# A hybrid encoder trunk on Trainium2: three edits to the order of queues around a retention stage

## The chip, the cores and the metric

The kernel runs on one core of one Trainium2 chip. A core has a matrix engine (TensorE, PE in the profile; PEld is its weight load), a vector engine (VectorE, DVE), a scalar engine (ScalarE, ACT), a general engine (GpSimd, POOL) and an engine that only issues transfers (SyncE, SP). Each works through its own list of instructions in order and waits on semaphores where an operand comes from another engine or from a transfer. The metric is the time of one execution on the device, in microseconds (us); several executions are timed and the median is given.

## The reference

Input is one sequence of 1024 frames with 1024 channels, in float32. The program has two layers, each x = x + mixer(RMSNorm(x)), and a last RMSNorm. The first layer projects h once and feeds two branches, whose gated outputs are joined by one output projection:

```python
proj = h @ w_in
u_s5, g_s5, q, k, v, g_ret = jnp.split(proj, cuts, axis=-1)
y = jax.nn.gelu(scan(u_s5))                      # S5 state-space branch
y = y * jax.nn.sigmoid(y @ glu_w + glu_b)        # its gate, a 1024 x 1024 product
y_s5 = y * jax.nn.silu(g_s5)
# retention: 8 heads, chunks of 64 frames, 64 key and 128 value channels a head
q, k = rope(q) * 64 ** -0.5, rope(k)
out = (q @ k.T * decay) @ v + (q * q_dec) @ S    # S: sum over earlier chunks of k.T @ v
out = (out - mean(out)) * rsqrt(var(out) + 1e-6) # per head
y_ret = out * jax.nn.silu(g_ret)
x = x + jnp.concatenate([y_s5, y_ret], axis=-1) @ w_out
```

(cut and shortened). The second layer is a convolution module: one projection into three parts, a causal depthwise convolution over 31 frames, a norm, and an output projection.

## The kernel before

Matrix products are made in three passes to keep float32 accuracy: each operand is split into a high part (a cast, `wh` for weights, `xh` or `yh` for data) and a low part (operand minus high part, `wl`, `xl`, `yl`), and TensorE adds high x high, low x high and high x low. A weight block comes in as one transfer (`wf`), ScalarE makes the cast, GpSimd or VectorE the subtraction. `wload_split` (L162 to L168) does it for the blocks of the value product and others, L266 to L269 for the gate's weights `glu0` to `glu7`.

The program is written in stages, and a scheduler turns them into one list per engine: it follows the order of writing and the priorities, but lets an instruction pass others that wait. `issue_after(x)` keeps all instructions written under it behind x, on x's own engine alone.

Three stages are touched. **The value product** (`ret_values`) goes over V_ORDER, seven products of combined weights; blocks are called V1_0, V1_1, V4_0 and so on (`mm_v` on TensorE, L1108 to L1110). Beside it `y_pass` (L942 to L945) takes the S5 output from DRAM (`yp`), applies the gelu on ScalarE (`yn`) and stores it to `yn_d`; these are the y norm passes, in the words of the change. Its instructions stand behind `last_sum`, the newest sum of a value product. **The key products** follow, and among them `y_operands` (L1071 to L1079), which loads the S5 output after the gelu again as eight blocks of two halves (`yf`), and splits them into `yh` and `yl`: these are the operands of the gate. **The retention** (`retention`, L947) goes over four pairs of heads. For a pair, `ret_turn` loads keys and queries from DRAM (`kraw`, `kswp`, `qraw`, `qswp` on SyncE), multiplies them by the rotary tables on GpSimd (L1004, L1006) and adds them on VectorE (L1014). `ret_heads` transposes the keys (`ktp`), decays them (`kt`), sums the states (`kv` on TensorE, `S` on VectorE), makes the scores (`sp`, masked into `sc`) and the outputs `ro0` and `ro1` of the two halves of the sequence, takes their mean and variance (`st`, `mv`), the root (`rs`, ScalarE), the normed `on` (VectorE), and transposes that back (`rt`), where it meets the gate `grl`, which is stored to `yr_d`. Names with two numbers carry the head and the half: `on_1_0` is head 1, first half.

While a pair is at work, two things are laid beside it. `glu_ahead` makes the S5 gate of the next block of 128 channels: a product of 24 matmuls a half (`mm_glu`), a tanh on ScalarE, the product `yg` on GpSimd (L1091) and the gated result on VectorE (L1095). And `weight_low` (L227 to L240) prepares low parts of weights that the second layer will need: a load (`lf`, L232), a cast on ScalarE (`lh`, L233), a subtraction on GpSimd (L234) and a store to DRAM (`lo`, L237). The four low parts of this stage, 20 to 23, have a single buffer each for `lf` and `lh`; the tuple H_LOWS says how many of them have been written when each pair begins.

## Time and profile before

| | |
|---|---|
| runs | 1177.71, 1180.71, 1185.98 us; median 1180.71 |
| profiled execution | 1179.18 us, its span from first to last instruction 1177.4 us |
| TensorE busy | 1155.9 us, 98% of the span; granted clock 0.997 on average |
| VectorE, GpSimd, ScalarE busy | 954.2, 718.3, 566.6 us (81%, 61%, 48%) |
| longest waits of TensorE | 2.4 us at `rt` of pair 0, 2.2 us at the first gate product, 2.1 us in two waits at later `rt`, 1.4 us in the value product |

Times in the views are microseconds from the start of the span. TensorE's waits are listed by the line that waited and the instruction that released it last; a stretch view gives busy time and the granted clock of the matrix engine in chosen windows. Rows of a time line say start, length, engine, line, operation and tiles; xN stands for N instructions in a row, and brackets hold the idle time ahead of the row and what ended it. A row "SPq" or "ACTq" is the issue of a transfer. The value product lies around 360 to 400 us, pair 0 of the retention begins near 500 us, pair 2 ends near 605 us.

### The profile page before, as it was taken

How to read it: one execution, taken by the hardware profiler on the slowest of the kernel's cores; microseconds unless marked ns; L12 is line 12 of the kernel's file. 1: busy time of each engine (PE TensorE's matmuls, PEld its weight loads, DVE VectorE, ACT ScalarE, POOL GpSimd, SP SyncE). 2: the span in 40 equal slices, each digit the busy share in tenths (PEclk: the TensorE clock that was granted, in tenths of full speed). 3: DMA queues.
4: the chain of work that ended last, by engine and by line, in shares of the span. 5: the costliest groups of instructions: out<-in, count | busy, mean ns of one | idle time of the engine just before them, and what ended most of it. 6: DMA issues, size and time to landing. Idle time of an engine off the chain costs nothing.

```text
span 1177.4 us, 17601 instructions
## 1 busy us (share of the span) xinstructions
PE 1155.9 (98%) x6102; PEld 958.2 (81%) x6102; DVE 954.2 (81%) x1541; ACT 566.6 (48%) x855; POOL 718.3 (61%) x499
## 2 busy tenths in 40 slices
PE   9999999999999999998999999999999999999997
PEld 7888788788887888877888788888888888888877
DVE  6889989999725666676888999579999999999643
ACT  7212342332236756413224846467756578544662
POOL 2049999888841143686532053439894689977742
PEclk9999999999999999999999999999999999999999
DMA  9359579877799979997676879975448653366863
GB/s 342 109 166 326 193 271 320 269 272 273 249 308 334 366 249 313 361 300 255 209 237 238 308 249 305 344 255 187 161 161 297 221 181 133 126 192 232 277 250 139
DMA packets 142137, 293.74 MB, mean 249 GB/s; under 512 B 14048, under 2 KB 42976, under 8 KB 141920
## 3 DMA queue, kind: packets, MB, share of 16 engines
q1 hardware_dynamic: 140896, 288.43, 72.2%
q10 hardware_dynamic: 1152, 4.19, 0.9%
q8 instruction: 48, 0.79, 0.3%
q14 instruction: 41, 0.34, 0.1%
HBM read 210.32 MB, written 81.20 MB: 248 GB/s over the span
## 4 chain that ended last, share of the span: by engine, by line
PE 70%; DVE 12%; DMA 10%; issue 3%; ACT 2%; SPq 1%; POOL 1%; DVEq 0%; ACTq 0%; POOLq 0%
PE mm_g L279 5%; PE mm_g L278 5%; PE mm_g L277 5%; PE mm_w L279 4%; PE mm_w L278 4%; PE mm_w L277 4%; PE mm_k L1026 4%; PE mm_a L279 2%; PE mm_b L278 2%; PE mm_a L278 2%; PE mm_b L279 2%; PE mm_a L277 2%; PE mm_b L277 2%; PE mm_oc L279 2%; PE mm_oc L278 2%
## 5 line engine op out<-in xcount | busy, mean ns | idle before, releaser
L1533 DVE SCALAR_TENSOR_TENSOR cv<-u,convw,cv 128x512 f32<-128x512 f32 x358 | 244.5, 748 | 4.5 <-ACT cv L1519 3.0
L1513 POOL TENSOR_TENSOR tp<-tp,tp 128x512 f32<-128x512 f32 x104 | 138.9, 1338 | 28.8 <-ACT tp L1512 23.5
L279 PE MATMUL mm_g<-xh,wl_g 128*128 128x512 f32 x256 | 100.8, 394 | 0.0
L278 PE MATMUL mm_g<-xl,wh_g 128*128 128x512 f32 x256 | 100.6, 393 | 0.0
L277 PE MATMUL mm_g<-xh,wh_g 128*128 128x512 f32 x256 | 100.4, 392 | 0.0
L1512 ACT ACTIVATE tp<-u,convw 128x512 f32<-128x512 f32 x104 | 69.8, 714 | 11.3 <-POOL tp L1513 11.0
L167 POOL TENSOR_TENSOR wl_K<-wf_K,wh_K 128x1024 fp32r<-128x1024 f32 x14 | 34.0, 2430 | 48.6 <-ACT wh_K L166 46.6
L278 PEld LDWEIGHTS mm_g<-xl,wh_g 128*128 128x128 f32 x256 | 48.1, 188 | 11.3 <-issue 1.6
L279 PEld LDWEIGHTS mm_g<-xh,wl_g 128*128 128x128 f32 x256 | 48.0, 188 | 10.5
L277 PEld LDWEIGHTS mm_g<-xh,wh_g 128*128 128x128 f32 x256 | 48.1, 188 | 9.6
L279 PE MATMUL mm_oc<-zh,wl_woc 128*128 128x512 f32 (+1 forms) x152 | 54.4, 359 | 0.6 <-DMA wl_woc<-lo_woc 0.6
L277 PE MATMUL mm_oc<-zh,wh_woc 128*128 128x512 f32 (+1 forms) x152 | 54.3, 361 | 0.0
L278 PE MATMUL mm_oc<-zl,wh_woc 128*128 128x512 f32 (+1 forms) x152 | 54.0, 356 | 0.0
L277 PE MATMUL mm_glu<-yh,wh_glu 128*128 128x512 f32 x128 | 51.2, 400 | 2.2 <-ACT yh L1270 2.2
L278 PE MATMUL mm_u<-xl,wh_u 128*128 128x512 f32 x128 | 50.0, 391 | 1.0 <-DVE xl L399 1.0
L278 PE MATMUL mm_glu<-yl,wh_glu 128*128 128x512 f32 x128 | 50.5, 394 | 0.2 <-DVE yl L1272 0.2
L279 PE MATMUL mm_glu<-yh,wl_glu 128*128 128x512 f32 x128 | 50.6, 396 | 0.0
L277 PE MATMUL mm_g<-h1h,wh_cg 128*128 128x512 f32 x128 | 50.3, 393 | 0.0
L277 PE MATMUL mm_a<-h1h,wh_ca 128*128 128x512 f32 x128 | 50.2, 392 | 0.0
L279 PE MATMUL mm_b<-h1h,wl_cb 128*128 128x512 f32 x128 | 50.2, 392 | 0.0
L279 PE MATMUL mm_a<-h1h,wl_ca 128*128 128x512 f32 x128 | 50.0, 390 | 0.0
L279 PE MATMUL mm_g<-h1h,wl_cg 128*128 128x512 f32 x128 | 49.8, 389 | 0.0
(834 smaller groups left out, 3671.9 us busy)
## 6 DMA issues: line engine op xcount, KB each, us to landing
wf_g<-w_ab SPq DMA_DIRECT2D x16, 512.0 KB, 6.2
a<-w_out SPq DMA_DIRECT2D x32, 256.0 KB, 4.5
ws<-a SPq DMA_DIRECT2D x32, 256.0 KB, 4.5
lf<-w_c SPq DMA_DIRECT2D x32, 256.0 KB, 5.1
wf_p<-ws SPq DMA_DIRECT2D x16, 512.0 KB, 4.8
wf_cb<-w_c SPq DMA_DIRECT2D x16, 512.0 KB, 5.0
wf_ca<-w_c SPq DMA_DIRECT2D x16, 512.0 KB, 4.8
wl_cb<-lo_cb SPq DMA_DIRECT2D x16, 512.0 KB, 3.3
```

The source lines that it names most:

```text
L167: e.tensor_tensor(wl[:].rearrange(fl), wf[:], wh[:].rearrange(fl).bitcast(F32), op=ALU.subtract)
L277: nc.tensor.matmul(ps, wh[:, kb, :], xh, start=start, stop=False, skip_group_check=chain)
L278: nc.tensor.matmul(ps, wh[:, kb, :], xl, start=False, stop=False, skip_group_check=chain)
L279: self.last_mm = nc.tensor.matmul(ps, wl[:, kb, :], xh, start=False, stop=stop, skip_group_check=chain)
L1026: self.last_mm = self.nc.tensor.matmul(ps, l[:, k, :], r[:], start=start and k == m == 0, stop=stop and k == 3 and m == 2, skip_group_chec ...
L1512: nc.scalar.mul(sk[:], u[:, k:k + HALF], cw[:, nb, k:k + 1])
L1513: gp.tensor_tensor(s0[:], s0[:], sk[:], op=ALU.add)
L1533: v.scalar_tensor_tensor(dst[:], *tap, accs_[i][:], op0=ALU.mult, op1=ALU.add)
```

## The change

Three edits. In `wload_split` the cast is kept as `last_cast`, and `y_pass` is written under `issue_after(last_cast)` beside `issue_after(last_sum)`: its gelu and its store on ScalarE's queue come behind the newest weight cast written so far. In `y_operands` the load is kept as `y_loaded`, and `ret_turn(pair + 1)` is written under `issue_after(y_loaded)`: SyncE issues the reload of the next pair's keys and queries behind the last load of a gate operand (only for the second pair are there such loads still to come). And H_LOWS goes from (0, 2, 4, 4) to (0, 0, 2, 4): low parts 20 and 21 are written beside the second pair instead of the first, 22 and 23 beside the third instead of the second.

```diff
--- before.py
+++ after.py
@@ -34,7 +34,7 @@
 LO_V = {f"g{i}" for i in range(1, 10)} | {"u4", "u5", "u6"}
 G0 = 3
 TP = 6
-LOWS, K_LOWS, V_LOWS, H_LOWS = 24, 20, 6, (0, 2, 4, 4)
+LOWS, K_LOWS, V_LOWS, H_LOWS = 24, 20, 6, (0, 0, 2, 4)
 NG = 4
 BLOCKS = ((4, 0), (4, 1), (0, 0), (0, 1), (1, 0), (1, 1), (5, 0), (5, 1), (2, 0), (2, 1), (3, 0), (3, 1), (6, 0), (7, 0), (6, 1), (7, 1))
 P_ORDER = ([(1, nb) for nb in range(4)] + [(2, nb) for nb in range(4)] +
@@ -163,7 +163,7 @@
         wh = self.wp.tile([P, KB, P], F32R, name=f"wh_{name}", tag="wh", bufs=3)
         wl = self.wp.tile([P, KB, P], F32R, name=f"wl_{name}", tag="wl", bufs=3)
         fl = "p k n -> p (k n)"
-        self.nc.scalar.copy(wh[:].rearrange(fl), wf[:])
+        self.last_cast = self.nc.scalar.copy(wh[:].rearrange(fl), wf[:])
         e.tensor_tensor(wl[:].rearrange(fl), wf[:], wh[:].rearrange(fl).bitcast(F32), op=ALU.subtract)
         return wh, wl
 
@@ -980,7 +980,8 @@
                     early.close()
                     self.lp = self.pool("l1", side="right")
             if pair < 3:
-                cur = self.ret_turn(pair + 1)
+                with self.tc.issue_after(self.y_loaded.ins):
+                    cur = self.ret_turn(pair + 1)
             self.ret_heads(pair, K, Q, qadds, V, turned)
             if pair < NG - 1:
                 self.glu_ahead(pair + 1)
@@ -1073,7 +1074,7 @@
 
         for kb in kbs:
             f = pool.tile([P, HALF], F32, name=f"yf{kb}_{h}", tag="xf", bufs=3)
-            self.nc.sync.dma_start(f[:], self.yn_d[kb * P:(kb + 1) * P, h * HALF:(h + 1) * HALF])
+            self.y_loaded = self.nc.sync.dma_start(f[:], self.yn_d[kb * P:(kb + 1) * P, h * HALF:(h + 1) * HALF])
             a, b = (self.op_tile(self.opA, f"A{h}", f"y{q}{kb}_{h}") for q in "hl")
             self.split(f[:], a, b, self.nc.vector)
             self.ys_in[h].append((a, b))
@@ -1148,7 +1149,7 @@
                     self.last_sum = scaled(d, h, b, ps[:], i in (3, 5))
                 for d, h in {5: ((0, 1),), 1: ((0, 0),), 6: ((0, 1),), 7: ((1, 0), (1, 1))}.get(i, ()):
                     self.last_sum = summed(d, h, b, ps[:])
-            with self.tc.issue_after(self.last_sum.ins):
+            with self.tc.issue_after(self.last_sum.ins), self.tc.issue_after(self.last_cast.ins):
                 for cb in (n - 1, n + 3) if 0 < n < 5 else ():
                     self.y_pass(vp, cb)
             with self.tc.issue_after(self.fetched.ins):
```

The scheduler's lists differ in more than these instructions. On ScalarE, in the value product, the rows below are before and then of the change (names as above; line numbers behind L982 are higher by one in the new file):

```order
L1122 CAST xh_2_1_171<-xf42_3616 128x512
L944 ACT_TABLE_LOAD
L944 ACTIVATE yn_0_3714<-yp_0_3712 128x1024
L166 CAST wh_V1_1_3680<-wf_V1_1_3678 128x1024
L945 DMA yn_d_87<-yn_0_3714 128x1024
L944 ACTIVATE yn_4_3719<-yp_4_3717 128x1024
L1122 CAST xh_3_1_181<-xf43_3620 128x512
L1122 CAST xth0_3600<-xf10_3624 128x512
L166 CAST wh_V4_0_3728<-wf_V4_0_3726 128x1024
L945 DMA yn_d_87<-yn_4_3719 128x1024
L1122 CAST xth1_3602<-xf11_3628 128x512
L166 CAST wh_V4_1_3758<-wf_V4_1_3756 128x1024
```

```order
L1123 CAST xh_2_1_171<-xf42_3616 128x512
L166 CAST wh_V1_1_3680<-wf_V1_1_3678 128x1024
L944 ACT_TABLE_LOAD
L944 ACTIVATE yn_0_3714<-yp_0_3712 128x1024
L944 ACTIVATE yn_4_3719<-yp_4_3717 128x1024
L1123 CAST xh_3_1_181<-xf43_3620 128x512
L945 DMA yn_d_87<-yn_0_3714 128x1024
L1123 CAST xth0_3600<-xf10_3624 128x512
L945 DMA yn_d_87<-yn_4_3719 128x1024
L1123 CAST xth1_3602<-xf11_3628 128x512
L166 CAST wh_V4_0_3728<-wf_V4_0_3726 128x1024
L166 CAST wh_V4_1_3758<-wf_V4_1_3756 128x1024
```

The cast of wh_V1_1 has moved ahead of the table load and the gelu of yp_0; the cast of wh_V4_0 has moved behind xth1, still behind both gelu passes.

On SyncE, at the end of the key products, before and then of the change (yf6_0 and yf7_0 are the last two gate operands, kraw_1 and kswp_1 the reload of the second pair):

```order
L1076 DMA yf6_0_4870<-yn_d_87 128x512
L1059 DMA kq_d_90<-qacc_2_4173 128x512
L998 DMA kraw_1_4997<-kq_d_90 128x1024
L1002 DMA kswp_1_4999<-kq_d_90 32x1024
L1076 DMA yf7_0_4876<-yn_d_87 128x512
L1002 DMA kswp_1_4999<-kq_d_90 32x1024 x2
L1059 DMA kq_d_90<-qacc_3_4175 128x512
L1002 DMA kswp_1_4999<-kq_d_90 32x1024
L266 DMA wf_glu4_5531<-w_glu 128x1024
```

```order
L1077 DMA yf6_0_4870<-yn_d_87 128x512
L1060 DMA kq_d_90<-qacc_2_4173 128x512
L1077 DMA yf7_0_4876<-yn_d_87 128x512
L999 DMA kraw_1_4983<-kq_d_90 128x1024
L1003 DMA kswp_1_4985<-kq_d_90 32x1024
L1060 DMA kq_d_90<-qacc_3_4175 128x512
L1003 DMA kswp_1_4985<-kq_d_90 32x1024 x3
L266 DMA wf_glu4_5519<-w_glu 128x1024
```

yf7_0 has passed kraw_1 and the first kswp_1; the store of qacc_3 has passed two of the other three kswp_1.

On VectorE, in pair 0 between the statistics of the first half and the norm of the second, before and then of the change (yg1_0 is the gated result of block 1 from the gate laid beside the pair):

```order
L564 RECIPROCAL rs_0_0_5114<-rs_0_0_5114 128x4
L1247 BN_AGGR mv_1_0_5123<-st_1_0_5122 128x2
L1252 TENSOR_SCALAR on_0_0_5117<-ro0_0_5088,mv_0_0_5105,rs_0_0_5114 128x128 x4
L564 RECIPROCAL rs_1_0_5132<-rs_1_0_5132 128x4
L1246 BN_STATS st_0_1_5158<-ro1_0_5140 128x6 x4
L1252 TENSOR_SCALAR on_1_0_5135<-ro0_1_5089,mv_1_0_5123,rs_1_0_5132 128x128 x4
L1247 BN_AGGR mv_0_1_5159<-st_0_1_5158 128x2
L1095 SCALAR_TENSOR_TENSOR yg1_0_5226<-mm_glu1_0_5231,yg1_0_5226 128x512
```

```order
L1096 SCALAR_TENSOR_TENSOR yg1_0_5212<-mm_glu1_0_5217,yg1_0_5212 128x512
L1248 BN_AGGR mv_1_0_5109<-st_1_0_5108 128x2
L564 RECIPROCAL rs_0_0_5100<-rs_0_0_5100 128x4
L1248 BN_AGGR mv_1_0_5109<-st_1_0_5108 128x2
L1253 TENSOR_SCALAR on_0_0_5103<-ro0_0_5074,mv_0_0_5091,rs_0_0_5100 128x128 x4
L564 RECIPROCAL rs_1_0_5118<-rs_1_0_5118 128x4
L1247 BN_STATS st_0_1_5144<-ro1_0_5126 128x6 x4
L1247 BN_STATS st_1_1_5162<-ro1_1_5127 128x6 x3
L1253 TENSOR_SCALAR on_1_0_5121<-ro0_1_5075,mv_1_0_5109,rs_1_0_5118 128x128 x4
```

yg1_0 stood behind on_1_0 and stands ahead of rs_0_0 and on_0_0 now; three of the four statistics st_1_1 have passed on_1_0. On TensorE the order of the stage differs by a few matmuls: five more of the gate stand ahead of rt of pair 0, and four fewer between ro1_5 and rt of pair 2. On SyncE the load lf_23 and the two stores lo_cb5 and lo_ca5 of lh_22 and lh_23 stand ahead of the stores yr_d of pair 1 (grl_3, grl_2) now; before, the low parts were done with by then. Nothing differs in the lists ahead of the value product's third block and behind the last gate of the retention.

## The prediction

> **What bounds the kernel now.** I read the busy times first: TensorE works through almost the whole span, so an edit can only win back what TensorE idles, or what it does at less than full speed.

> ```profile
> PE 1155.9 (98%) x6102; PEld 958.2 (81%) x6102; DVE 954.2 (81%) x1541; ACT 566.6 (48%) x855; POOL 718.3 (61%) x499
> ```

> The view of TensorE's waits (engine, line, what it waited for; us in total, times, longest) says where that idle time lies. The four longest rows are all at places that the change touches, in all 2.4 + 2.2 + 2.1 + 1.4 = 8.1 us.

> ```profile
> PE rt L1260 <- DVE mv L1247: 2.4, 1, 2.4
> PE mm_glu L277 <- ACT yh L1270: 2.2, 1, 2.2
> PE rt L1260 <- DVE on L1252: 2.1, 2, 1.2
> PE mm_v L1108 <- ACT wh_V L166: 1.4, 1, 1.4
> ```

> The third view is busy time by stretch of 3 us (stretch; sum and PE busy, instructions; granted clock; DMA share; GB/s). After the 2.2 us wait the clock is halved for a stretch (0.50) and only 10 instructions get through; after the 2.4 us wait it isn't (1.00).

> ```profile
> 506.00:509.00 3.00, 0.83 (x4) 0.95 1.03 350
> 509.00:512.00 3.00, 2.78 (x10) 0.50 0.72 213
> 536.00:539.00 3.00, 1.22 (x10) 1.00 0.89 313
> ```

> So the most that the change can reach is some 8.1 us and a half-clocked stretch of 3 us (1.5 us of work lost), 9.6 us. One per cent of the time, which is about what a measurement of this kernel can tell from no change, is 11.8 us. For each place the question is what is late next.

> **Term A, value product: the y norm behind the newest weight cast.** ScalarE first, then the consumer on TensorE and the next low part on GpSimd (start, us; in brackets the idle time before and its releaser):

> ```profile
> 361.49 2.01 ACT L1122 CAST xh<-xf 128x512 fp32r<-128x512 f32 x3 [6.91 <-DMA xf<-xt]
> 364.75 1.28 ACT L944 ACT_TABLE_LOAD   x1 [1.24 <-DMA yp<-y_d]
> 366.04 2.02 ACT L944 ACTIVATE yn<-yp 128x1024 f32<-128x1024 f32 x1
> 367.96 1.03 ACT L166 CAST wh_V<-wf_V 128x1024 fp32r<-128x1024 f32 x1
> ```
> ```profile
> 375.87 0.39 PE L1109 MATMUL mm_v<-wl_V,xh 128*128 128x512 f32 x1
> ```
> ```profile
> 373.02 2.41 POOL L167 TENSOR_TENSOR wl_V<-wf_V,wh_V 128x1024 fp32r<-128x1024 f32 x1 [28.08 <-ACT wh_V L166]
> ```

> The cast of wh_V1_1 stands behind the table load and the first y norm pass, which wait for yp. In the new order it runs from 363.50, where the three casts end, to 364.53, inside the 1.24 us that ScalarE idles anyway; the passes start no later, and nobody reads them until the y operands are loaded near 500 us. The wait of 1.4 us goes. Late next is wl_V4_0: its cast still stands behind two passes of 2.02 and three casts of 0.67 us (2.01 / 3). From 366.04 that is 372.1, and with its own 1.03 us 373.1, against 373.02 before. Its subtraction on GpSimd ends at 375.4 as now, where TensorE used it at 375.87 and would now want it 1.4 us earlier, at 374.5. A wait of 0.9 us takes the place of the one removed: 0.5 us are gained (bounds 0 and 1.4).

> **Term B, first gate of the S5 branch: the reload behind the last y operand.** TensorE waits for yh7_0, the cast of yf7_0. TensorE's last two matmuls ahead of the wait; SyncE's queue, whose first row is one of the two loads that now stand behind yf7_0's; the DMA view of 498 to 510 us (KB, us to landing); GpSimd and VectorE at yl7_0:

> ```profile
> 505.87 0.39 PE L278 MATMUL mm_glu<-yl,wh_glu 128*128 128x512 f32 x1
> 506.10 0.39 PE L279 MATMUL mm_glu<-yh,wl_glu 128*128 128x512 f32 x1
> ```
> ```profile
> 501.45 1.01 SPq L1002 DMA_DIRECT2D kswp<-kq_d  x1
> 502.55 0.38 SPq L1076 DMA_DIRECT2D yf<-yn_d  x1
> ```
> ```profile
> kraw<-kq_d SPq DMA_DIRECT2D x1, 512.0 KB, 3.7
> ...
> yf<-yn_d SPq DMA_DIRECT2D x1, 256.0 KB, 5.4
> ```
> ```profile
> 507.34 2.35 POOL L269 TENSOR_TENSOR wl_glu<-wf_glu,wh_glu 128x1024 fp32r<-128x1024 f32 x1
> ```
> ```profile
> 508.63 1.61 DVE L1272 TENSOR_TENSOR yl<-yf,yh 128x512 fp32r<-128x512 f32 x1 [3.62 <-ACT yh L1270]
> ```

> The load is issued at least 1.1 us earlier (502.55 - 501.45), and kraw's 512 KB are no longer ahead of it, which at the 350 GB/s of the stretch from 506 are at most 1.5 us. It lands not at 507.95 (502.55 + 5.4) but between 505.4 and 506.9, so yh7_0, with 0.6 for its cast, is there between 506.0 and 507.5; TensorE wants it at 506.33 (506.10 + one step of 0.23, 505.87 to 506.10). The wait of 2.2 becomes 0 to 1.2. yl7_0 is next. Before, its subtraction began while GpSimd's wl_glu2 ran and ended 0.55 us behind it, at 510.24. If it begins ahead of 507.34 it is through by then; if not, TensorE waits for it until 510.2 and little is gained.

> [...]

> The reload itself is hidden: GpSimd takes up kraw behind wl_glu2, at 509.7. What is won here at most is 2.2 + 1.5 = 3.7 us, but the retention of pair 0 doesn't move with it:

> ```profile
> 518.53 0.69 DVE L1095 SCALAR_TENSOR_TENSOR yg<-mm_glu,yg 128x512 f32<-128x512 f32 x1 [0.54 <-POOL yg L1091]
> ...
> 521.92 0.34 DVE L1197 SCALAR_TENSOR_TENSOR S<-S,g,kv 128x128 f32<-128x128 f32 x1
> ```
> ```profile
> 523.27 0.94 PE L1232 MATMUL ro<-S,qrot 64*128 64x128 f32 x11
> ```

> The state S of pair 0 is summed on VectorE behind this yg0_0, and yg0_0 waits for GpSimd, whose operations from 501 to 522 us run back to back in an unchanged order. TensorE reads S at 523.27, 1.0 us after its last part is there (521.92 + 0.34). So at 523 the gain of A and B together is capped near 1.0 us; I take 1.0 (bounds 0 and 3.7, the upper if GpSimd's chain starts earlier too).

> **Term C, rt of pair 0 (2.4 us).** No low parts stand beside pair 0 now:

> ```profile
> 531.66 0.62 ACT L233 CAST lh<-lf 128x512 fp32r<-128x512 f32 x1 [9.88 <-DMA lf<-w_c]
> ```
> ```profile
> 528.23 2.52 POOL L1006 TENSOR_TENSOR qswp<-qswp,ropek 128x512 f32<-128x512 f32 x2 [0.18 <-issue]
> ```
> ```profile
> 535.51 0.86 DVE L1246 BATCH_NORM_STATS2 st<-ro 128x6 f32<-128x128 f32 x4
> 536.28 1.35 DVE L1252 TENSOR_SCALAR on<-ro,mv,rs 128x128 f32<-128x128 f32 x4
> 537.55 0.17 DVE L1247 BATCH_NORM_AGGREGATE mv<-st 128x2 f32<-128x6 f32 x1
> 537.64 0.65 DVE L1095 SCALAR_TENSOR_TENSOR yg<-mm_glu,yg 128x512 f32<-128x512 f32 x1
> ```

> The cast of lh_21 held ScalarE for 9.88 us until its load landed, and behind it the table load and the root rs; that goes, and rs can be there 5 us earlier or more. But yg1_0 (the last row) now stands ahead of on_0_0 and on_1_0 on VectorE, and it needs GpSimd's product behind qswp_1: 528.23 + 2.52 = 530.75, plus half of the 2.52 for two, 532.0. From there yg1_0 0.65, on_0_0 1.35 as on_1_0, seven statistics rows (0.86 + 3 x 0.21 = 1.5), on_1_0 1.35: 536.9, with the two reciprocals and aggregates of 0.17 some 537.4, against 537.63 before (536.28 + 1.35). **A wait for GpSimd takes the place of the one removed.** What is gained beyond it is that five more gate matmuls (5 x 0.23 = 1.15 us) run ahead of rt, inside the wait. At this point 1.1 us in all are gained (bounds 0 and 3.5).

> **Term D, rt of the second half and pair 2.** The five matmuls are borrowed: of pair 2, the order has four fewer between ro1_5 and rt, so 0.9 us goes back there, and on_5_1 now comes behind two products of rt0 (2.47 / 4 = 0.62 each):

> ```profile
> 602.66 2.47 DVE L1263 TENSOR_TENSOR grl<-rt,grl 128x512 f32<-128x512 f32 x4
> 605.05 1.28 DVE L1170 TENSOR_TENSOR kt<-ktp,kdec 128x512 f32<-128x512 f32 x2
> 606.25 1.28 DVE L1014 TENSOR_TENSOR qrot<-qraw,qswp 128x512 f32<-128x512 f32 x2
> ```

> VectorE's own work up to kt of pair 3 is the same 1.35 + 2.47 + 1.28 in another order, and kt, which TensorE waits for, still ends it. I take 0.6 us given back of the 1.1 (bounds 0 and 2): the four fillers, less a part of the waits for on and kt that an earlier start leaves over. **Sum: 1.1 - 0.6 = 0.5 us gained**; A and B end at the cap ahead of C and are not added to it. The profiled execution took 1179.18 us, so 1178.7; it lies 1.5 under the median of the runs (1180.71), from which the same step gives 1180.2. I name 1179.4, between the two. Its own range, by the bounds, is 1176 to 1182.

> **Rivals.** *The stalls go as they show.* If wl_V4_0 isn't late and GpSimd's chain slides forward too, 1.4 + 3.7 + 2.4 = 7.5 us go, less the 0.9 given back: 6.6, or 1173. For it speaks that each of the three waits has one named releaser; against it the GpSimd rows above.

> *Slower: the low parts hold SyncE at pair 2.* Their casts and subtractions (0.6 and 1.3 us each) are as many as before, on engines that are busy 48 and 61%; what counts is their place. lh_22 and lh_23 move there, and the store of lh_23 now stands ahead of the stores of grl, behind which grl's and q's loads of pair 3 wait:

> ```profile
> 577.35 2.53 POOL L1006 TENSOR_TENSOR kswp<-kswp,ropek 128x512 f32<-128x512 f32 x2
> ```
> ```profile
> 594.24 2.52 POOL L1004 TENSOR_TENSOR qraw<-qraw,ropek 128x512 f32<-128x512 f32 x2 [12.00 <-DVE st L1246]
> ```
> ```profile
> 582.70 1.34 SPq L1266 DMA_DIRECT2D yr_d<-grl  x2
> 587.61 0.32 SPq L1220 DMA_DIRECT2D grl<-gr_d  x1
> 588.02 0.38 SPq L998 DMA_DIRECT2D qraw<-kq_d  x1
> ```

> lh_22's subtraction runs behind kswp_3 (579.88 + 1.29), its store lets lf_23 out at 581.6; 5.4 us to land (as yf), 0.6 for the cast, 1.3 on GpSimd: 588.9 instead of 582.70. Then qraw_3 goes out near 594 instead of 588.02, GpSimd starts on it 6.2 us on (594.24 - 588.02), and four of its steps of 1.26 (2.53 / 2) bring it to 605; VectorE reaches qrot_3 at 606.25. One us is left. Each us beyond it is one on the time: if the two loads take 2 us longer each, TensorE waits 3 us for qrot_3, and 1178.7 becomes 1181.7. It decides from the moment that qraw_3 is issued after 595.

> *The clock gate.* At rt of pair 0 a gap of 2 us or more remains, and the 2.2 us gap cost a half-clocked stretch while the 2.4 us gap did not. If it strikes there, 1.5 us are lost: 1180.2 from the profiled time. [...]

> *The change does nothing measurable in its own place,* because the order decides otherwise: 1179.2; the listing of the order speaks against it.

> **How the numbers follow.** Forecast 0.5; stalls gone 0.13; SyncE held 0.20; clock 0.12; nothing 0.05. None reaches one per cent alone; the last per cents are for a shift of the later stages that I don't see. The executions before spread from 1177.7 to 1186.0, so the range runs from 1174.5 to 1185.0. Faster by over 1%: 0.03, within 1%: 0.89, slower: 0.08.

> **What would show it.** Right: the wait for wh_V gone and one for wl_V in its place; the 2.2 us wait for yh gone and no half-clocked stretch at 509; rt of pair 0 still waiting some 2 us, for VectorE behind GpSimd. Wrong: no wait at rt of pair 0 (then C was undersized), or a new wait for qrot at sp of pair 3 (then SyncE was held).

## The result: slower by 0.4%, with the profile after

The changed kernel takes 1184.89 us (median of 22 runs, 1181.85 to 1191.41), the kernel before 1180.62 us beside it. The ratio is 1.0044, 95% interval 1.0032 to 1.0056. That lies inside one per cent, which the prediction took for what can be told from no change; with this many runs the interval is 0.12% to either side and shows the loss. It lies inside the stated range by 0.1 us, which is luck: that range was widened to the spread of single runs, and the one worked out from the terms, 1176 to 1182, is missed. Forecast were 1179.4 and a gain of 0.5 us; 4.3 us are lost. The profiled execution took 1187.44 us (span 1185.7), 2.6 above its median, where the profiled one before lay 1.4 below its own; so the traces differ by 8.3 us and the medians by 4.3.

TensorE's waits in the changed kernel (line, what it waited for; us in total, times, longest):

```profile
PE ro L1233 <- DVE sc L1211: 5.7, 2, 5.5
PE rt L1261 <- DVE on L1253: 4.6, 2, 3.1
...
PE mm_v L1110 <- POOL wl_V L167: 0.8, 1, 0.8
```

The waits for wh_V (1.4 us), for yh (2.2) and for mv at rt of pair 0 (2.4) are gone. In their place stand a wait for wl_V of 0.8, one for `on` at rt of pair 0 of 1.5 (4.6 less 3.1), one for `on` at rt of pair 2 that grew from 1.2 to 3.1, and a new one of 5.5 us that no term of the prediction has: TensorE's outputs ro1 of pair 3 wait for masked scores, `sc`.

The stretch view of the changed kernel (stretch; sum, then busy us and instructions of PE, PEld, DVE, ACT, POOL; granted clock, DMA share, GB/s):

```profile
506.00:509.00 3.00, 3.00 (x19) 2.61 (x18) 2.45 (x4) 1.55 (x2) 3.00 (x2) 1.00 0.83 272
...
600.00:602.00 2.00, 1.62 (x10) 1.62 (x11) 1.12 (x4) 0.90 (x1) 2.00 (x2) 0.73 0.00 0
602.00:604.00 2.00, 2.00 (x14) 1.67 (x14) 1.68 (x3) 0.00 (x0) 2.00 (x2) 0.50 0.00 0
604.00:606.00 2.00, 2.00 (x32) 1.83 (x31) 1.96 (x5) 0.00 (x0) 0.42 (x1) 0.91 0.72 33
...
618.00:621.00 3.00, 2.10 (x15) 1.88 (x15) 2.02 (x4) 0.00 (x0) 1.27 (x1) 0.50 1.02 333
621.00:624.00 3.00, 3.00 (x14) 3.00 (x15) 3.00 (x21) 0.59 (x2) 0.00 (x0) 0.50 1.06 403
624.00:627.00 3.00, 3.00 (x15) 2.56 (x14) 2.04 (x9) 0.00 (x0) 1.86 (x2) 0.86 0.24 92
```

The first gate is full and at full clock now. The halved clock has moved: behind the 3.1 us wait, and for longer behind the 5.5 us wait.

**Where the gain went.** Each matmul was set against the same matmul of before (start after less start before): -0.2 us at 367 us, ahead of the first place that the change touches, -3.0 at the first ro of pair 0, -2.5 at rt of pair 0, -3.4 through pairs 1 and 2, -2.4 at the second rt of pair 2, -2.6 at the last scores of pair 3; then +3.1 at ro1 of pair 3, +6.3 at the first rt of pair 3, +6.6 to +8.1 in the first block of the output projection behind it, +8.9 at 742 us, and no more after that (+8.3 at the end). The change does win about 3 us where it was expected to act. Between ro1 (612.89 us) and the first rt of pair 3 (631.24) it loses these and 6.3 us more, and 2.6 beyond that in the first blocks of the output projection.

**The chain behind the 5.5 us wait**, in the changed kernel. SyncE's queue from the two low parts on, then GpSimd, VectorE and TensorE:

```profile
585.36 0.33 SPq L237 DMA_DIRECT2D lo_ca<-lh  x1
585.78 0.88 SPq L1267 DMA_DIRECT2D yr_d<-grl  x2
...
589.56 0.39 SPq L999 DMA_DIRECT2D qraw<-kq_d  x1
...
604.45 0.35 SPq L159 DMA_DIRECT2D wf_p<-w_out  x1
604.90 0.85 SPq L1267 DMA_DIRECT2D yr_d<-grl  x2
610.16 0.32 SPq L1221 DMA_DIRECT2D grl<-gr_d  x1
610.54 0.42 SPq L1319 DMA_DIRECT2D yg<-gs_d  x1
```
```profile
597.17 2.49 POOL L1005 TENSOR_TENSOR qraw<-qraw,ropek 128x512 f32<-128x512 f32 x2 [11.84 <-DMA qraw<-kq_d]
...
602.08 2.35 POOL L269 TENSOR_TENSOR wl_glu<-wf_glu,wh_glu 128x1024 fp32r<-128x1024 f32 x1
616.25 1.26 POOL L1322 TENSOR_TENSOR yg<-yg,yn 128x512 f32<-128x512 f32 x1 [11.83 <-DMA yg<-gs_d]
```
```profile
617.55 0.69 DVE L1327 SCALAR_TENSOR_TENSOR sg<-sg,yg 128x512 f32<-128x512 f32 x1 [8.34 <-POOL yg L1322]
618.16 0.68 DVE L1211 TENSOR_TENSOR sc<-sp,retmask 128x512 f32<-128x512 f32 x1
619.82 0.69 DVE L1327 SCALAR_TENSOR_TENSOR sg<-sg,yg 128x512 f32<-128x512 f32 x1 [0.98 <-POOL yg L1322]
620.43 0.68 DVE L1211 TENSOR_TENSOR sc<-sp,retmask 128x512 f32<-128x512 f32 x1
```
```profile
618.90 2.07 PE L1233 MATMUL ro<-S,qrot 64*128 64x128 f32 x14 [5.53 <-DVE sc L1211]
```

The same rows of the kernel before, where ro1 didn't wait:

```profile
601.62 0.35 SPq L159 DMA_DIRECT2D wf_p<-w_out  x1
604.57 0.92 SPq L1266 DMA_DIRECT2D yr_d<-grl  x2
607.28 0.32 SPq L1220 DMA_DIRECT2D grl<-gr_d  x1
```
```profile
599.22 2.38 POOL L269 TENSOR_TENSOR wl_glu<-wf_glu,wh_glu 128x1024 fp32r<-128x1024 f32 x1
613.14 3.12 POOL L1321 TENSOR_TENSOR yg<-yg,yn 128x512 f32<-128x512 f32 x2 [11.54 <-DMA yn<-yn_d]
```
```profile
614.44 0.69 DVE L1326 SCALAR_TENSOR_TENSOR sg<-sg,yg 128x512 f32<-128x512 f32 x1 [3.39 <-POOL yg L1321]
615.05 1.28 DVE L1210 TENSOR_TENSOR sc<-sp,retmask 128x512 f32<-128x512 f32 x2
```

Read it as one chain, with the delay against before at each link. The last store of a low part (lo_ca) holds the stores of grl: 585.78 against 582.70, 3.1 us late. The queries of pair 3 go out 1.5 us late (589.56 against 588.02); they take 7.5 us to land instead of 6.1, so GpSimd, which waits for them, starts 2.9 late, and so does wl_glu7 behind them. The next weight load on SyncE, wf_p1_2, waits for a buffer and is 2.8 us late; it stands ahead of the next stores of grl. Before, these waited for VectorE's products; now the products are done in time, but the stores stand behind wf_p1_2. They go out only 0.3 late, yet 0.45 us behind a load of 512 KB instead of 2.95 us, and the load of grl_7, which needs their buffer, follows after 5.3 us instead of 2.7 (610.16 - 604.90; 607.28 - 604.57). So yg4, the first operand of the gate stage behind the retention (L1319 to L1327), is 2.9 us late, and its result sg4 on VectorE 3.1. The last two masked scores of pair 3, which have nothing to do with yg4, stand behind the first sg4 in VectorE's list in both kernels; in the change the very last one stands behind the second sg4 too. Before, that cost nothing. Now TensorE arrives 2.6 us earlier and the scores come 3.1 us later: 5.7 us against the measured wait of 5.5. The clock is then at half from 618 to 624.84 (0.14 x 3 / 0.5 = 0.84 us of the last stretch); TensorE works from 618.90, so about 3.0 us of work are lost, which is the step from +3.1 to +6.3.

### The profile page after: what moved, and what is told of

The parts are those of the page before. It is cut to its first block, busy times and chain, and to the rows that moved or that the text cites. A ratio compares the mean times of both kernels' runs of the same rounds, so it can differ in the third digit from the quotient of the medians.

```text
span 1185.7 us, 17597 instructions
## 1 busy us (share of the span) xinstructions
PE 1160.2 (98%) x6102; PEld 961.5 (81%) x6102; DVE 952.7 (80%) x1541; ACT 566.0 (48%) x855; POOL 719.9 (61%) x499
## 4 chain that ended last, share of the span: by engine, by line
PE 74%; DMA 12%; DVE 8%; issue 3%; ACT 2%; SPq 1%; POOL 1%; DVEq 0%; ACTq 0%; POOLq 0%
PE mm_g L278 6%; PE mm_g L279 6%; PE mm_g L277 6%; PE mm_w L279 3%; PE mm_w L277 3%; PE mm_w L278 3%; PE mm_oc L277 2%; PE mm_oc L278 2%; PE mm_oc L279 2%; PE mm_a L279 2%; PE mm_a L277 2%; PE mm_b L277 2%; PE mm_a L278 2%; PE mm_b L278 2%; PE mm_b L279 2%
## 5 line engine op out<-in xcount | busy, mean ns | idle before, releaser
L279 PE MATMUL mm_g<-xh,wl_g 128*128 128x512 f32 x256 | 100.8, 394 | 0.0
L278 PE MATMUL mm_g<-xl,wh_g 128*128 128x512 f32 x256 | 100.6, 393 | 0.0
L277 PE MATMUL mm_g<-xh,wh_g 128*128 128x512 f32 x256 | 100.5, 392 | 0.0
L167 POOL TENSOR_TENSOR wl_K<-wf_K,wh_K 128x1024 fp32r<-128x1024 f32 x14 | 34.0, 2429 | 48.4 <-ACT wh_K L166 39.2
L278 PEld LDWEIGHTS mm_g<-xl,wh_g 128*128 128x128 f32 x256 | 48.1, 188 | 11.3 <-issue 1.6
L279 PEld LDWEIGHTS mm_g<-xh,wl_g 128*128 128x128 f32 x256 | 48.0, 188 | 10.6
L277 PEld LDWEIGHTS mm_g<-xh,wh_g 128*128 128x128 f32 x256 | 48.1, 188 | 9.6
L279 PE MATMUL mm_oc<-zh,wl_woc 128*128 128x512 f32 (+1 forms) x152 | 54.4, 359 | 0.0
L277 PE MATMUL mm_oc<-zh,wh_woc 128*128 128x512 f32 (+1 forms) x152 | 54.3, 361 | 0.0
L278 PE MATMUL mm_oc<-zl,wh_woc 128*128 128x512 f32 (+1 forms) x152 | 54.0, 356 | 0.0
L277 PE MATMUL mm_glu<-yh,wh_glu 128*128 128x512 f32 x128 | 51.1, 399 | 0.5 <-DVE yg L1096 0.5
L278 PE MATMUL mm_u<-xl,wh_u 128*128 128x512 f32 x128 | 50.0, 391 | 0.9 <-DVE xl L399 0.9
L277 PE MATMUL mm_g<-h1h,wh_cg 128*128 128x512 f32 x128 | 50.3, 393 | 0.0
L279 PE MATMUL mm_glu<-yh,wl_glu 128*128 128x512 f32 x128 | 50.3, 393 | 0.0
L277 PE MATMUL mm_a<-h1h,wh_ca 128*128 128x512 f32 x128 | 50.2, 392 | 0.0
L279 PE MATMUL mm_b<-h1h,wl_cb 128*128 128x512 f32 x128 | 50.2, 392 | 0.0
L278 PE MATMUL mm_glu<-yl,wh_glu 128*128 128x512 f32 x128 | 50.2, 392 | 0.0
L279 PE MATMUL mm_a<-h1h,wl_ca 128*128 128x512 f32 x128 | 50.0, 390 | 0.0
L279 PE MATMUL mm_g<-h1h,wl_cg 128*128 128x512 f32 x128 | 49.8, 389 | 0.0
## 6 DMA issues: line engine op xcount, KB each, us to landing
wf_g<-w_ab SPq DMA_DIRECT2D x16, 512.0 KB, 6.4
a<-w_out SPq DMA_DIRECT2D x32, 256.0 KB, 4.4
ws<-a SPq DMA_DIRECT2D x32, 256.0 KB, 5.0
lf<-w_c SPq DMA_DIRECT2D x32, 256.0 KB, 5.0
wf_p<-ws SPq DMA_DIRECT2D x16, 512.0 KB, 4.8
wf_cb<-w_c SPq DMA_DIRECT2D x16, 512.0 KB, 4.9
wf_ca<-w_c SPq DMA_DIRECT2D x16, 512.0 KB, 4.8
wl_cb<-lo_cb SPq DMA_DIRECT2D x16, 512.0 KB, 3.5
```

The lines of the kernel that those rows point to most:

```text
L167: e.tensor_tensor(wl[:].rearrange(fl), wf[:], wh[:].rearrange(fl).bitcast(F32), op=ALU.subtract)
L277: nc.tensor.matmul(ps, wh[:, kb, :], xh, start=start, stop=False, skip_group_check=chain)
L278: nc.tensor.matmul(ps, wh[:, kb, :], xl, start=False, stop=False, skip_group_check=chain)
L279: self.last_mm = nc.tensor.matmul(ps, wl[:, kb, :], xh, start=False, stop=stop, skip_group_check=chain)
```

## The experiments

All ratios are to the kernel before, run beside them on the same chip; they are not the ratio of the two medians, and differ from it most where the times of a kernel lie in two groups (e6). The lines stand in order of what they tell apart; low parts are given as in H_LOWS, how many have been written when pairs 0, 1, 2, 3 begin.

| run | what | median us | ratio, 95% interval |
|---|---|---|---|
| the change | 0,0,2,4 | 1184.89 | 1.0044, 1.0032 to 1.0056 |
| e1 | change, low parts as before | 1179.57 | 1.0003, 0.9986 to 1.0021 |
| e2 | before, low parts of the change | 1188.69 | 1.0069, 1.0038 to 1.0101 |
| e3 | before, cast edit alone | 1180.70 | 1.0007, 0.9987 to 1.0027 |
| e4 | before, load edit alone | 1179.23 | 0.9999, 0.9980 to 1.0018 |
| e13 | before, 0,2,2,4 | 1181.08 | 1.0000, 0.9986 to 1.0014 |
| e14 | before, 0,0,4,4 | 1184.34 | 1.0032, 1.0013 to 1.0051 |
| e5 | change, 0,0,4,4 | 1182.74 | 1.0032, 1.0016 to 1.0048 |
| e16, e15 | all four in the key products; before, change | 1191.48, 1192.53 | 1.0093 (1.0072 to 1.0114), 1.0105 (1.0082 to 1.0129) |
| e7 | change, last low part stored by ScalarE's queue | 1187.17 | 1.0052, 1.0034 to 1.0069 |
| e10 | change, yg4 loads on ScalarE's queue | 1183.54 | 1.0018, 1.0002 to 1.0035 |
| e12 | before, yg4 loads on ScalarE's queue | 1181.05 | 1.0001, 0.9988 to 1.0014 |
| e6 | change, sg4 behind the scores | 1185.33 | 1.0023, 1.0003 to 1.0042 |
| e9 | change, grl products behind the last on | 1183.47 | 1.0014, 1.0000 to 1.0027 |
| e11 | e9 and e10 | 1181.64 | 1.0007, 0.9993 to 1.0021 |
| e17 | e9 and e6 | 1180.67 | 1.0009, 0.9994 to 1.0025 |
| e8 | e5 and e6 | 1181.60 | 1.0014, 0.9999 to 1.0029 |
| e18 | e5 and e9 | 1181.98 | 1.0021, 1.0003 to 1.0038 |

### Which of the three edits

e1 is the change with the tuple put back, e2 the kernel before with the tuple alone:

```diff
-LOWS, K_LOWS, V_LOWS, H_LOWS = 24, 20, 6, (0, 0, 2, 4)
+LOWS, K_LOWS, V_LOWS, H_LOWS = 24, 20, 6, (0, 2, 4, 4)
```

> The change with H_LOWS put back to (0, 2, 4, 4); the y norm behind the newest cast and the reload behind the last y operand stay. Theory S (the low parts 22 and 23 beside the third pair hold SyncE, so that what pair 3 needs comes late): the 5.5 us wait for sc at ro1 of pair 3 and the 3.1 us wait at rt of pair 2 go; the time falls below the change by 4 to 6 us and lies 0 to 2 us under the kernel before (1178.5 to 1180.5). Rival T (the start of pair 3 is set by something that does not depend on the low parts, and whatever is won in the value product and at the first gate turns into a wait there): a wait of 2 to 4 us at pair 3 stays, and the time is the kernel before's or slower.

> The kernel before with H_LOWS (0, 0, 2, 4) alone. Theory S: the wait for sc at ro1 of pair 3 is there with 3 to 6 us, and the time is 4 to 7 us over the kernel before, as far or further than the change (1184 to 1187). Rival T: the stage of the first gate isn't earlier here, so pair 3 has no wait of its own, and the time is within 2 us of the kernel before.

e3 is the kernel before with the cast edit, e4 the one with the load edit:

```diff
-            with self.tc.issue_after(self.last_sum.ins):
+            with self.tc.issue_after(self.last_sum.ins), self.tc.issue_after(self.last_cast.ins):
```
```diff
-                cur = self.ret_turn(pair + 1)
+                with self.tc.issue_after(self.y_loaded.ins):
+                    cur = self.ret_turn(pair + 1)
```

> The kernel before with the y norm passes behind the newest weight cast alone. Expected by the prediction's term A: the 1.4 us wait for wh_V goes, one of 0.7 to 1.2 us for wl_V of V4_0 stands in its place, 0.5 us are gained in that stage and swallowed at the first gate or at rt of pair 0: within 0.1% of the kernel before. Rival (the wait goes without another in its place): 1.4 us less at the end of the value product.

> The kernel before with the reload behind the last y operand alone. Theory: the 2.2 us wait for yh and the half-clocked stretch behind it go (some 3.5 us at the first gate), but rt of pair 0 still waits for the root behind lh_21, so the wait there grows from 2.4 us to 4 or 5 us, and the time stays within 0.1% of the kernel before. Rival (what is won at the first gate is kept): 2 to 3.5 us faster than the kernel before (ratio 0.997 to 0.998).

The low parts carry the whole loss: without them 1.0003, alone 1.0069. The two other edits do what was read of them in their own place and are worth nothing that can be measured. In e3 the wait for wh_V is replaced by one for wl_V, in e4 the wait for yh is gone and the one at rt of pair 0 has grown from 2.4 to 2.8 us, less than the 4 or 5 that were expected; the waits of e3, then of e4:

```profile
PE mm_v L1109 <- POOL wl_V L167: 1.0, 1, 1.0
```
```profile
PE rt L1261 <- DVE mv L1248: 2.8, 1, 2.8
```

In e2 the wait for sc at ro1 is there as well, with 6.2 us and without any earlier start from the other edits. Its seven runs lie in two groups, two at 1181.3 to 1181.5 and five at 1187.8 to 1193.2, and the trace is of the second:

```profile
PE ro L1232 <- DVE sc L1210: 6.2, 1, 6.2
PE rt L1260 <- DVE on L1252: 3.1, 1, 3.1
```

### Which place of the low parts

e13 (before, 0,2,2,4) puts only the last two low parts beside the third pair; e14 (before) and e5 (change) have 0,0,4,4, all four beside the second pair (the second diff is that of e14):

```diff
-LOWS, K_LOWS, V_LOWS, H_LOWS = 24, 20, 6, (0, 2, 4, 4)
+LOWS, K_LOWS, V_LOWS, H_LOWS = 24, 20, 6, (0, 2, 2, 4)
```
```diff
-LOWS, K_LOWS, V_LOWS, H_LOWS = 24, 20, 6, (0, 2, 4, 4)
+LOWS, K_LOWS, V_LOWS, H_LOWS = 24, 20, 6, (0, 0, 4, 4)
```

> The change with H_LOWS (0, 0, 4, 4): all four low parts beside the second pair, none beside the first or the third. The order on TensorE and VectorE is that of the change to the last instruction (sg4_1 still ahead of the last sc, on_5_1 still behind the products of rt0); only the places of lh_22 and lh_23 on SyncE, ScalarE and GpSimd differ, and the store of lh_23 no longer stands ahead of the stores of grl_3 and grl_2. Theory S (the hold of SyncE makes pair 3 late): those stores go out near 580, qraw_3 near 585, yg4_0 is loaded 3 us earlier or more, the 5.5 us wait for sc falls under 2 us and the time under the kernel before: 1176 to 1180. Rival V (VectorE's order, sg4_1 ahead of sc, is enough): the wait for sc stays at 3 us or more and the time at 1183 or more.

> The kernel before with H_LOWS (0, 2, 2, 4): low parts 20 and 21 stay beside the first pair, 22 and 23 move from the second to the third. VectorE's order is the kernel before's at rt of pair 2 and in pair 3; TensorE's in pair 3 too. Theory X (the transfers and steps of 22 and 23 in the third pair, by themselves, bring qraw_3, wl_glu7 and yg4 late): the load of yg4_0 goes out 2 us or more later than 607.65, a wait for sc of 2 to 4 us stands at ro1 of pair 3, and the time is 2 to 4 us over the kernel before (ratio 1.002 to 1.0035). Theory Y (the order that the scheduler makes with no low parts in pair 0 is what costs): within 0.1% of the kernel before.

> The kernel before with H_LOWS (0, 0, 4, 4): none beside the first pair, all four beside the second, none beside the third. VectorE has the order of the change (yg1_0 ahead of on_0_0, on_5_1 behind the products of rt0, sg4_1 ahead of the last sc). Theory X: the wait at ro1 of pair 3 is under 1.5 us, 3 us stay at rt of pair 2, and the time is 0 to 2 us over the kernel before. Theory Y: as slow as the change with H_LOWS alone, 5 us or more over the kernel before.

e13 holds the stores of grl exactly as long as the change does, and costs nothing that can be measured:

```profile
585.77 1.75 SPq L1266 DMA_DIRECT2D yr_d<-grl  x2
```

Its profiled run has no wait at ro1 of pair 3: TensorE reaches the last scores of that pair at 613.64, 4.5 us later than in the change, and covers the delay. In e2, where all four low parts come later, the same stores go out at 590.86, 5.1 us later than here, and nothing covers that. So a hold of 3 us on SyncE is not the loss by itself; it takes a longer hold or an earlier TensorE. e14 and e5 have no such hold and lose 0.3% all the same, more than Theory S of e5 and Theory X of e14 allowed, though the wait at ro1 of pair 3 is small in both (0.8 and 0.6 us), as they said. The waits of e5:

```profile
PE rt L1261 <- DVE on L1253: 4.3, 2, 3.1
PE sp L1205 <- DVE S L1198: 2.7, 2, 1.7
PE ro L1233 <- DVE sc L1211: 1.3, 3, 0.8
```

The 1.7 us wait at sp is one of pair 1, which has all four low parts beside it here. In these two traces pair 1 gives back more than any other place, from its first ktp to its last rt: 2.4 us in e5 and 2.9 in e14, where the change, with two low parts there, gives back 0.3. So e5 and e14 lose in a place of their own, and are no clean test of VectorE's order alone.

The 3.1 us wait at rt of pair 2 is in each of these kernels (3.10 in e5 and e14, 3.11 in e6, e10 and the change). VectorE's row for it in the change:

```profile
597.79 1.26 DVE L1264 TENSOR_TENSOR grl<-rt,grl 128x512 f32<-128x512 f32 x2
598.97 1.36 DVE L1253 TENSOR_SCALAR on<-ro,mv,rs 128x128 f32<-128x128 f32 x4
```

on_5_1 stands behind two of the products of rt0, as term D had it, and the second rt waits for it. All the kernels with nothing beside pair 0 have this order, but for those whose edit moves these products.

In e15 (change) and e16 (before) the question was the other way: none of the four beside any pair.

```diff
-LOWS, K_LOWS, V_LOWS, H_LOWS = 24, 20, 6, (0, 0, 2, 4)
+LOWS, K_LOWS, V_LOWS, H_LOWS = 24, 24, 6, (0, 0, 0, 0)
```

> The change with all four low parts written in the key products (K_LOWS 24, H_LOWS all zero), so that none stands beside any pair. Theory X: no wait over 1.5 us at ro1 of pair 3; with the stalls of the value product and the first gate gone too, 0 to 3 us under the kernel before (1177 to 1180). Rival (the key products, where the transfer engines are busy, lose what is won here): 1181 or more.

> The kernel before with all four low parts written in the key products, without the two other edits. Theory X: the 2.4 us wait at rt of pair 0 shrinks, no wait at pair 3: 0 to 2 us under the kernel before, and 1 us or so behind e15 if the two other edits are worth anything once no low part stands beside the pairs.

Both lose 10 to 11 us. The low parts then stand in SyncE's queue in the key products, ahead of the gate's operands: yf7_0 goes out at 506.44 in e16 against 502.55 before, and the first gate waits for the yl (e15):

```profile
PE mm_glu L278 <- DVE yl L1273: 5.0, 5, 2.0
```

The key products had no room for them; what was asked of the pairs can't be read from these two runs.

### Which link of the chain

e7 takes the store of the last low part off SyncE's queue:

```diff
-        self.nc.sync.dma_start(self.lo_d[key][:, c], hi[:].bitcast(F32))
+        (self.nc.scalar if k == 23 else self.nc.sync).dma_start(self.lo_d[key][:, c], hi[:].bitcast(F32))
```

> The change with one issue moved: the store of lh_23 goes out on ScalarE's queue instead of SyncE's; nothing else differs on any engine. Theory S: the stores of grl_3 and grl_2 go out when wl_glu6 is done, at 583.3 instead of 585.8, every later step of that chain 2.5 us earlier, and the wait for sc falls from 5.5 to about 3 us; 2 to 4 us won against the change: 1181 to 1183. Rival V: nothing changes (1184 to 1186).

A miss. The stores of grl are issued 1.7 us earlier (584.06 against 585.78), but end no earlier, since they take longer by as much and more; the transfers issued from 580 to 595 us (KB, median us to landing), in e7 and then in the change:

```profile
yr_d<-grl SPq DMA_DIRECT2D x2, 512.0 KB, 6.1
```
```profile
yr_d<-grl SPq DMA_DIRECT2D x2, 512.0 KB, 3.8
```

grl_5 is loaded at 589.20 against 589.15 and the wait at ro1 stays (5.7). The store that moved, 256 KB, takes longer as well: 5.5 us to landing from ScalarE's queue against 2.5 from SyncE's. In these two traces the other issuer saved time of issuing and no more.

e10 puts the loads that are late, those of yg4 and of its yn, on ScalarE's queue, past everything that waits on SyncE; e12 does it to the kernel before (in part; the load of yn is changed in the same way):

```diff
-            nc.sync.dma_start(yg[:], self.gs_d[rows(nb), hs(h)])
+            q = nc.scalar if nb == NG else nc.sync
+            q.dma_start(yg[:], self.gs_d[rows(nb), hs(h)])
```

> The change with the four loads of yg4 and yn4 on ScalarE's queue, where they stand ahead of the table load before sg4_0 and don't wait for grl_7's load and, by it, for the stores of grl_5 and grl_4 on SyncE. (The scheduler also puts the last scores ahead of sg4_0 then.) Theory: yg4_0 is there by 605 to 608 instead of 617.5, the wait for sc at ro1 of pair 3 goes whole, and the kernel keeps only the wait at rt of pair 2: 1179 to 1181. Rival (pair 3 waits for something else by then, as q or the states): a wait of 3 us or more stays in pair 3, 1183 or more.

> The kernel before with the four loads of yg4 and yn4 on ScalarE's queue alone. Theory: TensorE has no wait at ro1 of pair 3 before, so nothing is won there: within 0.15% of the kernel before. Rival (these loads also set the time of the kernel before): 1 to 3 us faster.

The wait at ro1 goes. The first loads of yg4 are early now, and the scheduler has put the masked scores ahead of the first sg4 besides, so e10 alone can't tell the late loads from the order. But the first rt of pair 3 waits 4.1 us. The last of the four loads, yn of the second half, goes out at 615.35, later than in the change (613.55). VectorE stands idle for 7.3 us at the product of that half, sg4_1, and the statistics of pair 3 and both `on` stand behind it; TensorE and VectorE in e10:

```profile
629.57 1.94 PE L1261 MATMUL rt<-ident,on 128*128 128x128 f32 x8 [4.09 <-DVE on L1253]
```
```profile
621.98 0.69 DVE L1328 SCALAR_TENSOR_TENSOR sg<-sg,yg 128x512 f32<-128x512 f32 x1 [7.27 <-POOL yg L1323]
...
628.08 1.34 DVE L1253 TENSOR_SCALAR on<-ro,mv,rs 128x128 f32<-128x128 f32 x4
```

The wait passed from the first half of sg4 to the second. To the kernel before, which had no wait at ro1, the same edit does nothing (e12).

e6 leaves the loads as they are and mends VectorE's order at pair 3: sg4 behind the last masked scores. e9 mends it at pair 2: the products of rt behind the pair's last `on` (at every pair; the last `sc` of pair 3 is then ahead of the second sg4 again, too). e11 is e9 with e10, e17 is e9 with e6; e8 and e18 are e6 and e9 on e5. The edits of e6 and then of e9, in part:

```diff
-            v.scalar_tensor_tensor(sg[:], sg[:], 1.0, yg[:], op0=ALU.add, op1=ALU.mult)
+            with self.tc.issue_after(self.masked[1].ins) if nb == NG else nullcontext():
+                v.scalar_tensor_tensor(sg[:], sg[:], 1.0, yg[:], op0=ALU.add, op1=ALU.mult)
```
```diff
-                    v.tensor_tensor(gts[hh][:, c], tp[:], gts[hh][:, c], op=ALU.mult)
+                    with self.tc.issue_after(last_on.ins):
+                        v.tensor_tensor(gts[hh][:, c], tp[:], gts[hh][:, c], op=ALU.mult)
```

> The change with the two gated results sg4_0 and sg4_1 written behind the last masked scores of pair 3 on VectorE; SyncE's order up to there stays that of the change, so the loads of yg4 are as late as in it. Theory S, second half (the late yg4 reaches TensorE only through VectorE's order): the wait for sc at ro1 of pair 3 goes, and 5 us or more are won against the change: 1177 to 1181. Rival (the scores themselves, the states or q of pair 3 are late too): a wait of 3 us or more stays at ro or sp of pair 3.

> The change with the products of the gate grl written behind the last normed on of their pair on VectorE: on_5_1 ahead of the products of rt0 again, and by that also the last sc of pair 3 ahead of sg4_1, both as in the kernel before; SyncE, GpSimd and ScalarE as in the change up to pair 3's end. Theory (three costs: the order at rt of pair 2 some 1 us, the late yg4 in front of sc0 some 3 us, sc1 behind sg4_1 some 1.5 us with the slow clock after it): the 3.1 us wait at rt of pair 2 falls to 1.2, the wait at ro1 of pair 3 stays at 2 to 4 us since sc0_3 is behind sg4_0 in both orders: 1181 to 1184. Rival V (VectorE's order is all): both waits go, 1178 or less.

> Both e5 and e6: all low parts beside the second pair, and sg4 behind the last masked scores. If each cures the same wait, no more than the better of the two: 1176 to 1179, 2 to 4 us under the kernel before. If they cure different waits, 2 us more.

> Both e9 and e10. Theory: no wait of pair 3, 1.2 us at rt of pair 2; what the change wins at the first gate and in pair 0 (about 2 to 3 us) is left: 1176 to 1179, a little under the kernel before. Rival: no better than the kernel before (1180 or more), since the gain in pair 0 is lost again elsewhere.

> The change with both of VectorE's orders mended: the three grl products of the pair stand behind the last `on` (so that on_5_1 is ahead of the products of rt0 again), and the two sg4 behind the last masked scores of pair 3. The two orders apart gave 1.0014 (the products moved) and 1.0023 (sg4 moved), against 1.0044 for the change. Theory: the two waits, 3.1 us at rt of pair 2 and 5.5 us at ro1 of pair 3, are two separate costs, so with both gone the ratio is 1.000 to 1.001 and the first matmul of mm_w comes within 2 us of that of the kernel before. Rival: the yg4 loads are what is late, whatever VectorE's order, so the wait passes to the next tile that needs them (on_7_0 or the y gate of pair 3) with 3 us or more, and the ratio stays at 1.002 or above.

> The change with the low parts 22 and 23 beside the second pair of heads again, 0,0,4,4, and the grl products behind the last `on`. Without the second edit 0,0,4,4 gave 1.0032 and a wait of 3.1 us at rt of pair 2. Theory: that wait falls to about 2.1 us, and the ratio to 1.001 to 1.0025, since the smaller waits at sp of pair 1 and in mm_w are left. Rival: the wait at rt of pair 2 costs nothing by itself, since what is gained there is waited for at ro1 of pair 3, which grows to 2 us or more, and the ratio stays at 1.003.

With sg4 behind the scores (e6, e8) nothing is left of the wait at ro1 of pair 3, so the order on VectorE is what lets late loads reach TensorE there. The runs of e6 fall into two groups, 1178.6 to 1180.5 (five) and 1184.9 to 1187.7 (seven); what parts them is not known, and its trace is of the second. With the products behind the last `on` (e9) TensorE is 3.9 us ahead of the kernel before up to pair 3, and waits all the more at ro1, 6.2 us. Each mend alone leaves part of the loss (1.0023 and 1.0014); only the interval of e9 lies clear of that of the change. The two together (e17) bring it to 1.0009, an interval that reaches 1 and does not touch that of the change. The forecasts of e17 and e18 came out; e9 had its time but neither of its waits; e6, e8, e10 and e11 were forecast 2 us or more too low. TensorE and VectorE in e17:

```profile
600.05 1.09 PE L1261 MATMUL rt<-ident,on 128*128 128x128 f32 x8 [2.13 <-DVE on L1253]
...
612.71 1.16 PE L1233 MATMUL ro<-S,qrot 64*128 64x128 f32 x16
```
```profile
609.96 1.29 DVE L1211 TENSOR_TENSOR sc<-sp,retmask 128x512 f32<-128x512 f32 x2 [1.66 <-PE sp L1205]
613.50 0.69 DVE L1329 SCALAR_TENSOR_TENSOR sg<-sg,yg 128x512 f32<-128x512 f32 x1 [2.25 <-POOL yg L1323]
```

The scores no longer follow sg4 and ro1 starts without a wait, 2.8 us earlier than before (615.46 there). The early gain isn't kept as time, though: 1.0009 is no gain. Of the mechanisms, then: the two places on VectorE together account for the loss within the intervals. How much of it each carries is not settled, since the intervals of e6, e9, e8 and e18 overlap. Where the lead of e17 goes, its trace shows: 2.8 us at ro1, 2.1 at rt of pair 3 and at the first matmul of the output projection, none 5 us behind that, and 0.7 at the end of the span. In between TensorE waits 1.0 us for ysh, 0.6 for ysl and 0.2 for wh_p, where the kernel before has 0.5 for wl_p alone: the next place where another engine sets the pace. That is one trace, and the runs of the two kernels overlap (1176.6 to 1184.4; 1175.8 to 1183.5). No version beats the kernel before by more than its interval.

## Why the prediction was wrong, point by point

**Term A was right** in kind, and near in size. The wait for wh_V is replaced by one for wl_V of 0.8 us (0.9 was said); this is the matmul of the changed kernel:

```profile
374.64 0.50 PE L1110 MATMUL mm_v<-wl_V,xh 128*128 128x512 f32 x1 [0.84 <-POOL wl_V L167]
```

Behind it the shift is -1.1 us, and at 367 us, just ahead of the place, it was -0.2: 0.9 gained, 0.5 said (bounds 0 and 1.4).

**Term B was right on the wait and wrong on its cap.** No wait for yh and no halved clock, as the test named. Of the two cases for yl7_0 the first came: it runs from 503.22 to 504.81, ahead of wl_glu2, which begins at 505.91. Both cases are in the trace of before: a yl begun at 464.89, while GpSimd's wl_K ran, ended at 467.19, 0.55 us behind it (466.64), and took 2.30; one begun at 489.27, 0.15 us ahead of a wl_glu, took 0.68. But the cap of 1.0 us at ro of pair 0 rested on GpSimd's chain staying where it was. It didn't: its first operation in the stretch starts at 499.18 against 501.10, and yg0_0 comes at 516.67 against 518.53.

```profile
516.67 0.69 DVE L1096 SCALAR_TENSOR_TENSOR yg<-mm_glu,yg 128x512 f32<-128x512 f32 x1 [0.54 <-POOL yg L1092]
```

With it the sums of S and ro0 come earlier (520.20 against 523.16, the first matmul of ro), so 3.0 us were gained at this point, inside the bounds (0 and 3.7) and near the end that was not taken. "Back to back in an unchanged order" doesn't hold a chain in place when its first link starts earlier. Where the chain stays, the cap holds: in e4 GpSimd takes up kraw at 509.61, as before (509.65), and the shift at ro is 1.0 us more than at the value product.

**Term C was right in kind, short in size.** rt of pair 0 waits for `on` on VectorE:

```profile
535.26 0.95 PE L1261 MATMUL rt<-ident,on 128*128 128x128 f32 x7 [1.53 <-DVE on L1253]
```

1.53 us instead of some 2, with the five gate matmuls ahead of it. 2.5 us were gained here against 1.1, since GpSimd's product for yg1_0, forecast for 532.0, was there by 530.14.

**Term D was short.** The place was right, and so was its cause, on_5_1 behind the products of rt0. It gave back 1.0 us (-3.4 to -2.4) against 0.6; the wait of 3.11 us is 1.9 longer than before, less the 0.9 of the four matmuls.

**Up to pair 3 the sum was thus better than forecast**, 2.6 us gained against 0.5. What failed is one step of the second rival, *"the low parts hold SyncE at pair 2"*. It named the right hold and then priced it at one consumer, qrot_3: "It decides from the moment that qraw_3 is issued after 595." The hold was shorter than worked out there (the stores of grl at 585.78, not 588.9), qraw_3 was issued at 589.56 and qrot_3 was in time; by that price the rival was worth nothing, and it had 0.20. The forecast itself put the hold at nothing, and neither of the signs that were to show it wrong appeared. But the queue that is held goes on behind q's loads, through the buffer of wl_glu7, the load wf_p1_2, the stores of grl and the load of grl_7 to yg4, and none of these links was followed. Nor was VectorE's list of pair 3 read, where sg4 stands ahead of scores that don't need it. There the delay meets TensorE: 5.5 us of wait and some 3.0 us of work lost at the halved clock behind it, where the sum had nothing. The chance of a loss was seen; its place, its size and its sign in the forecast were not.

The runs also say that this hold was only part of it. e13 has the hold without the loss, and e9, which leaves the low parts where the change has them and mends VectorE's order, loses 0.1% instead of 0.4%. Taking the low parts off pair 0 changes that order at pair 2 and at the last scores of pair 3; term D saw the first, at 0.6 us, and nothing saw the second. e14 and e5 lose 0.3% without the hold, but not by that order alone: pair 1, with four low parts beside it, gives back more in their traces (2.9 and 2.4 us) than rt of pair 2 (1.0). The clock rival was priced at the wrong place: the halved clock came not at rt of pair 0, where 1.5 us remained to wait, but at pairs 2 and 3.

## What to carry to other kernels

Follow a held queue to its end: the instruction behind the one that was moved is not its last consumer, and the price falls due where a late transfer meets an engine's list in which something urgent stands behind something that isn't. A gain ahead of such a place is no gain; TensorE arrives earlier and waits longer (in e9 3.9 us earlier, for a wait of 6.2), so before adding up terms look for the next place where another engine sets the pace. And moving work off a busy stage moves it into another: in e14 the freed pair gained 2.3 us, and the pairs behind it gave back 3.9.
